# A diffusion layer's token mixer: the rows of a small inverse placed in other slots, one direction's preparation a slot later, the weights' remainders on GpSimd

## The chip, the core and the metric

The kernel runs as one program on one core of a Trainium2 chip. The engines of a core work side by side, each through its own instructions in a fixed order: TensorE (PE; its weight loads are a row of their own, PEld), VectorE (DVE), ScalarE (ACT), GpSimd (POOL) and SyncE (SP), which issues nearly all the DMAs here. The metric is the device time of one execution in microseconds; lower is better. Each variant is timed in several runs, and one execution is also recorded by the profiler.

## The reference, cut to what matters

All data is float32. One layer is computed for 256 latent tokens (x) and 256 context tokens, width 2048:

```
x, cx = LN(alpha*x + 1/2*gate0*SwiGLU_a(mod0(x))),  the same for the context
h   = mod1(x), mod1(cx)
p   = h @ w_in                        # RWKV-7 part (3328 columns) and gMLP part (2048)
for d in (0, 1):                      # forward and backward over the tokens
    S_t = S_{t-1}(diag(w_t) + a_t^T b_t) + v_t^T k_t ;  y_t = S_t r_t     # 16 heads of 64
out = concat(group_norm(y_0 + y_1)..., gMLP(p)) @ w_out
x   = LN(alpha*x + gate1*out);  x = LN(alpha*x + 1/2*gate2*SwiGLU_b(mod2(x)))
```

## The kernel before, in words

The kernel has three long stages: the first SwiGLU, the mixer, the second SwiGLU. Every large product is made of three float32r products: a weight piece `raw` from HBM is rounded on ACT to `whi` (L299), the remainder `wlo` = raw - whi is formed (L302), and TensorE adds whi·h_hi, whi·h_lo and wlo·h_hi (L311 to L313). `wsplit` (L287) does the loading and splitting; a piece is 128x512. There are three `raw` buffers, each of two pieces, and four `whi` and four `wlo` (RAWB, HIB). A list `turn` says who forms `wlo`: with `turn[1]` = 0 always DVE, with 2 every second piece GpSimd, with 1 every piece GpSimd. From the end of the first SwiGLU on and in the mixer's recurrence it is 2; behind the recurrence it is set to 1.

In the mixer the recurrence is done in chunks of 64 tokens by matrices, for a tile t of two heads (eight tiles) and a direction d. The 16 pairs are the units u = 2t + d. The loop over u runs three chains side by side:

- `finish(u)`: `solve`, then for d = 1 group norm and output of the tile. `solve` begins with `pu`, which needs the inverse `R` of its unit (L939); then come `pg` (with `gi`, `wc` on DVE), `pq` (with `qy`), and seven state steps, each a product `pS` on TensorE and an update `S` on DVE (L1004, L1011) that the next one needs.
- `begin(u + 2)`: the preparation of a later unit (`prologue` for d = 0 alone, then `prep`): a scan `pf` on DVE, exponentials `e`, `ei` on ACT, `kd`, `nb`, `bk`, `ar`, `wn` on DVE and `bk`, `ar`, `ac`, `kdx` on GpSimd, products `px`, the masked `aa`, `pt`, `pak`, eight small DMAs to `scr` and one of 1 MB from there to `abc`.
- `inverse(u + 1)`: the inverse of a 64x64 triangle per chunk and head. `small_inverse` makes the 16x16 blocks, row by row: 15 rows, each a product (`a`, L851) and a sum (`x`, L852) on DVE, every row needing the one before. Then `Rt`, `R1`, and the products `pX`, `pR`, `pX2`, `pR2`, with `Z`, `R1`, `R` copied by DVE and ACT between them.

`together` takes one step (up to the next `yield`) of every chain in turn, and after each such pass, a slot, calls `burst`: some of the products still owed for coming tiles (`project`: `pp`; the gMLP's `gmlp_v`: `pgv`, and `gmlp_u`: `pu`; later `wout`: `pwo`) are issued. So a `yield` is where large products may go between steps of the chains. Code that stands in a `behind()` is put after the most recent `urgent` instruction. The order on each engine is then fixed when the program is built; it need not be that of the code.

In a loop pass with d = 1, `finish` takes 13 slots (0 to 12), in one with d = 0 the preparation takes 11 or 12. The lines that the change touches are L734, L853, L859 and, ahead of the loop over u, L1303. Lines behind L734 have numbers higher by 2 or 3 in the changed kernel.

Of the kernel before, what the change touches and what calls it, by code (L numbers as in the profile page):

```python
# [43 lines left out]
def fl(ap):  # L44
    names = " ".join(f"a{i}" for i in range(len(ap.shape) - 1))
    return ap.rearrange(f"p {names} -> p ({names})")
# [7 lines left out]
def tile_layer(ctx: ExitStack, tc: tile.TileContext, x, c, ctx_in, c_ctx, w_ada, b_ada, ln_g, ln_b,  # L54
# [16 lines left out]
    def ps_v(name):  # L71
        return psum.tile([P, 512], F32, tag="v", name=name, bufs=3)
# [7 lines left out]
    def pre(name, shape=(P, 512), dt=F32):  # L80
        return sp.tile(list(shape), dt, tag="pre", name=name, bufs=PRES)
# [7 lines left out]
    def own(name, shape=(P, 512), dt=F32, bufs=1):  # L89
        return sp.tile(list(shape), dt, tag=name, name=name, bufs=bufs)  # L90
# [196 lines left out]
    turn = [0, 0]  # L287
# [413 lines left out]
    def behind():  # L701

        return tc.issue_after(urgent[0].ins) if urgent[0] is not None else nullcontext()
# [11 lines left out]
    def prep(t, d, k, r, kk, vt, ups, kdx, s):  # L715
# [15 lines left out]
        with behind():  # L731
            nc.vector.tensor_reduce(zp[:, :, 0], zp[:, :, 1:L // 2 + 1], axis=AX.X, op=ALU.add, negate=True)
            nc.vector.tensor_tensor_scan(fl(pf), fl(m65), fl(zp), 0.0, op0=ALU.mult, op1=ALU.add)
        yield  # L734
        sgn = -KAPPA if d == 0 else KAPPA
        e = pre("e", (P, NCH, L + 1))
        nc.scalar.activation(fl(e), fl(pf), AF.Exp, scale=sgn)
# [103 lines left out]
    def small_inverse(d, s):  # L841

        x = own("x16", (P, 8, 16), bufs=2)
        sub = own("a16", (P, 8, 16))
        for z in (x, sub):
            nc.scalar.copy(z, i16.unsqueeze(1).to_broadcast([P, 8, 16]))
        for n, i in enumerate(range(14, -1, -1) if d == 0 else range(1, 16)):
            lo, hi = (i + 1, 16) if d == 0 else (0, i)
            r = slice(i, 16) if d == 0 else slice(0, i + 1)
            with behind():  # L850
                nc.vector.tensor_tensor(sub[:, :, lo:hi], x[:, :, lo:hi], s["abc"][:, i, :, lo:hi], op=ALU.mult)  # L851
                nc.vector.tensor_reduce(x[:, :, i], sub[:, :, r], axis=AX.X, op=ALU.add)  # L852
            if n % 4 == 3:  # L853
                yield
        s["x16"] = x

    def inverse(d, s):

        aa = s["aa"]  # L859
        for _ in range(2):  # L860
            yield
        yield from small_inverse(d, s)

        Rt = own("Rt", (P, 8, 32))
        nc.vector.tensor_tensor(Rt.rearrange("p j (b t) -> p j b t", t=16), s["x16"].unsqueeze(2).to_broadcast([P, 8, 2, 16]),
                                mh[:, 0, :].unsqueeze(1).unsqueeze(3).to_broadcast([P, 8, 2, 16]), op=ALU.mult)
        R1 = own("R1", (P, 8, 32))
        nc.vector.transpose(R1, Rt)
        yield
        yield  # L870
        pX = ps_v("pX")
        for i in range(8):
            for b in range(4):
                sb = slice(32 * b, 32 * b + 32)
                nc.tensor.matmul(pX[sb, 32 * i:32 * i + 32], aa[sb, b // 2, i // 4, i % 4, 32 * (b % 2):32 * (b % 2) + 32],
                                 Rt[sb, i, :], start=True, stop=True)
        Z = own("Z", (P, 8, 32))
        urgent[0] = nc.vector.tensor_tensor(Z, pX[:, 0:256].rearrange("p (i t) -> p i t", t=32),
                                ml[d].unsqueeze(1).to_broadcast([P, 8, 32]), op=ALU.mult)
        yield  # L880
        pR = ps_v("pR")
        for i in range(8):
            for b in range(4):
                sb = slice(32 * b, 32 * b + 32)
                nc.tensor.matmul(pR[sb, 32 * i:32 * i + 32], Z[sb, i, :], R1[sb, i, :], start=True, stop=True)
        nc.vector.tensor_tensor(fl(R1), pR[:, 0:256], fl(R1), op=ALU.add)

        Rt = own("Rt", (P, 8, 32))
        nc.vector.transpose(Rt, R1)
        R = own("R", (P, 8, L))  # L890
        nc.vector.tensor_tensor(R.rearrange("p j (b t) -> p j b t", t=32), R1.unsqueeze(2).to_broadcast([P, 8, 2, 32]),
                                mh[:, 1, :].unsqueeze(1).unsqueeze(3).to_broadcast([P, 8, 2, 32]), op=ALU.mult)
        fa, fb = (0, 32) if d == 0 else (32, 0)
        yield
        pX = ps_v("pX2")
        for i in range(8):
            for q in range(2):
                sa, sb = slice(64 * q + fa, 64 * q + fa + 32), slice(64 * q + fb, 64 * q + fb + 32)
                nc.tensor.matmul(pX[sb, 32 * i:32 * i + 32], aa[sa, q, i // 4, i % 4, fb:fb + 32], Rt[sa, i, :],
                                 start=True, stop=True)  # L900
        Z = own("Z", (P, 8, 32))
        for q in range(2):
            sb = slice(64 * q + fb, 64 * q + fb + 32)
            pz = pX[sb, 0:256].rearrange("p (i t) -> p i t", t=32)
            if q:
                nc.scalar.copy(Z[sb], pz)
            else:
                nc.vector.tensor_copy(Z[sb], pz)
        yield
        pR = ps_v("pR2")  # L910
        for i in range(8):
            for q in range(2):
                sa, sb = slice(64 * q + fa, 64 * q + fa + 32), slice(64 * q + fb, 64 * q + fb + 32)
                nc.tensor.matmul(pR[sa, 32 * i:32 * i + 32], Z[sb, i, :], R1[sb, i, :], start=True, stop=True)
        for q in range(2):
            sa = slice(64 * q + fa, 64 * q + fa + 32)
            pz = pR[sa, 0:256].rearrange("p (i t) -> p i t", t=32)
            if q:
                nc.scalar.copy(R[sa, :, fb:fb + 32], pz)
            else:  # L920
                nc.vector.tensor_copy(R[sa, :, fb:fb + 32], pz)
        s["R"] = R
# [348 lines left out]
    def put(g):  # L1271
        queue.append(g)
        return g
# [22 lines left out]
    put(gate_low())  # L1296
    gens[1, 2] = put(project(1, 2))
    together(begin(1), inverse(0, unit[0]))
    begun(1)
    gm = []  # L1300
    for cb in range(4):
        gm += [gmlp_v(cb), gmlp_u(2 * cb), gmlp_u(2 * cb + 1)]
    nu = 2 * NRT  # L1303
    for u in range(nu):
        t, d = u // 2, u % 2
        pace[0] = left[0] / (nu - u + REST) / SLOTS
        if t + 2 < NRT:
            for i in ((0, 2) if d == 0 else (1,)):
                gens[t + 2, i] = put(project(t + 2, i))
            put(gm.pop(0))  # L1310
        if u == 12:
            drain()
            put(tail())
        chains = [finish(u)]
        if u + 2 < nu:
            if d == 0:
                for i in range(3):
                    drain(gens[t + 1, i])
            chains.append(begin(u + 2))
        if u + 1 < nu:  # L1320
            chains.append(inverse((u + 1) % 2, unit[u + 1]))
        together(*chains)
        if u + 2 < nu:
            begun(u + 2)
# [219 lines left out]
```

## Time and profile before

| | us |
|---|---|
| median of three runs | 3366.95 (3363.61 to 3374.13) |
| the profiled execution | 3355.58 |
| its span, from the first to the last instruction | 3353.9 |
| TensorE busy in the span | 3180.8 (95%) |
| VectorE | 2111.1 (63%) |
| ScalarE | 1265.4 (38%) |
| GpSimd | 437.1 (13%) |

The profiled execution was 11.4 us shorter than the median of the runs. Its own time is 1.7 us longer than its span. Busy shares are means over three stages that have different limits; the loop over the units is one part of the span (about 1795 to 2560 us), and what is read of it is read there.

### The profile page before, as it was taken

To read this page: it belongs to the slowest core of one execution; us is meant where nothing else is said; L and a number is where in the kernel's file an instruction comes from. 1 tells how busy PE (TensorE), PEld (TensorE's weight loads), DVE (VectorE), ACT (ScalarE), POOL (GpSimd) and SP (SyncE) were. 2 spreads that over 40 slices of the span, in tenths; PEclk is the share of its full clock that TensorE was granted. 3 is DMA by queue.
4 is the path that set the end of the run, shared out by engine and by line. 5 is a ranking of instruction groups with operands and counts; after the bars stand their busy time and mean duration, and the time that the engine had idled before them with its cause. 6 is when DMAs were issued, how large, how long until landed. Compare 5 with 4: busy or idle time off the path is not lost. (4 is left out here: it accounts for less than half of the span.)

```text
span 3353.9 us, 55585 instructions
## 1 busy us (share of the span) xinstructions
PE 3180.8 (95%) x21224; PEld 2537.6 (76%) x21224; DVE 2111.1 (63%) x4253; ACT 1265.4 (38%) x2225; POOL 437.1 (13%) x393
## 2 busy tenths in 40 slices
PE   8999999999999999999888988898898999999997
PEld 3556877787878878788787777777787888888886
DVE  2345676967557565533867667666776756656568
ACT  2321222222222222222464444544443554444443
POOL 2100000000000000000463333333323000000003
PEclk9999999999999999999988999998898999999999
DMA  8866465757647566433354353434553766666664
GB/s 289 271 201 203 146 177 158 215 168 232 195 145 234 155 192 195 129 94 100 114 158 124 98 120 97 111 97 110 127 128 105 227 209 194 188 189 189 190 188 148
DMA packets 562515, 554.36 MB, mean 165 GB/s; under 512 B 42383, under 2 KB 415284, under 8 KB 560200
## 3 DMA queue, kind: packets, MB, share of 16 engines
q1 hardware_dynamic: 561800, 550.61, 55.0%
q8 instruction: 167, 2.74, 0.3%
q14 instruction: 100, 0.82, 0.1%
q0 software_dynamic: 384, 0.17, 0.0%
q10 hardware_dynamic: 64, 0.02, 0.0%
HBM read 543.35 MB, written 7.35 MB: 164 GB/s over the span
## 5 line engine op out<-in xcount | busy, mean ns | idle before, releaser
L299 ACT CAST whi<-raw 128x512 fp32r<-128x512 f32 (+1 forms) x1366 | 839.4, 618 | 1707.6 <-PE po L312 352.4
L302 DVE TENSOR_TENSOR wlo<-raw,whi 128x512 fp32r<-128x512 f32 (+1 forms) x1188 | 826.2, 698 | 687.8 <-ACT whi L299 678.1
L302 POOL TENSOR_TENSOR wlo<-raw,whi 128x512 fp32r<-128x512 f32 x178 | 240.9, 1356 | 2491.0 <-ACT whi L299 2464.7
L311 PE MATMUL po<-ahi,whi 128*128 128x512 f32 (+1 forms) x768 | 292.6, 381 | 3.8 <-DVE X L417 3.1
L313 PE MATMUL po<-ahi,wlo 128*128 128x512 f32 (+1 forms) x768 | 291.1, 379 | 3.6 <-DVE wlo L302 3.6
L312 PE MATMUL po<-alo,whi 128*128 128x512 f32 (+1 forms) x768 | 292.3, 381 | 0.0
L311 PE MATMUL pgate<-h,whi 128*128 128x512 f32 x704 | 277.9, 395 | 2.0 <-ACT h L307 1.6
L311 PE MATMUL pup<-h,whi 128*128 128x512 f32 x704 | 278.0, 395 | 0.9 <-ACT whi L299 0.9
L313 PE MATMUL pup<-h,wlo 128*128 128x512 f32 x704 | 275.3, 391 | 1.0 <-DVE wlo L302 0.9
L313 PE MATMUL pgate<-h,wlo 128*128 128x512 f32 x704 | 275.1, 391 | 0.2 <-DVE wlo L302 0.2
L312 PE MATMUL pgate<-h,whi 128*128 128x512 f32 x704 | 274.7, 390 | 0.0
L312 PE MATMUL pup<-h,whi 128*128 128x512 f32 x704 | 274.5, 390 | 0.0
L417 DVE SCALAR_TENSOR_TENSOR X<-po,modc,X 128x256 f32<-128x256 f32 x352 | 155.1, 479 | 155.4 <-PE po L313 150.4
L274 DVE SCALAR_TENSOR_TENSOR vt<-xk,wa,vt 128x512 f32<-128x512 f32 x256 | 187.3, 748 | 30.2 <-DMA xk<-in_w_ada_dram 28.5
L311 PEld LDWEIGHTS po<-ahi,whi 128*128 128x128 f32 x768 | 145.9, 190 | 43.3 <-issue 7.7
L274 DVE SCALAR_TENSOR_TENSOR vt<-xv,wa,vt 128x512 f32<-128x512 f32 x224 | 163.7, 748 | 23.2 <-DMA xv<-in_w_ada_dram 21.7
L311 PEld LDWEIGHTS pgate<-h,whi 128*128 128x128 f32 x704 | 132.1, 188 | 53.7 <-ACT whi L299 12.2
L312 PEld LDWEIGHTS po<-alo,whi 128*128 128x128 f32 x768 | 146.0, 190 | 35.2 <-issue 7.5
L311 PEld LDWEIGHTS pup<-h,whi 128*128 128x128 f32 x704 | 132.2, 188 | 51.7 <-ACT whi L299 14.9
L313 PEld LDWEIGHTS po<-ahi,wlo 128*128 128x128 f32 x768 | 146.1, 190 | 33.0 <-DVE wlo L302 4.2
L311 PE MATMUL pp<-h,whi 128*128 128x256 f32 (+1 forms) x448 | 158.6, 354 | 4.1 <-ACT whi L299 2.9
L313 PE MATMUL pp<-h,wlo 128*128 128x256 f32 (+1 forms) x448 | 152.9, 341 | 5.2 <-POOL wlo L302 2.6
(389 smaller groups left out, 6264.0 us busy)
## 6 DMA issues: line engine op xcount, KB each, us to landing
raw<-in_ffn_b_wi_dram SPq DMA_DIRECT2D x176, 512.0 KB
raw<-in_ffn_a_wi_dram SPq DMA_DIRECT2D x156, 512.0 KB
xv<-in_w_ada_dram SPq DMA_DIRECT2D x256, 256.0 KB
xk<-in_w_ada_dram SPq DMA_DIRECT2D x256, 256.0 KB
raw<-in_w_in_dram SPq DMA_DIRECT2D x110, 512.0 KB
raw<-in_ffn_a_wo_dram SPq DMA_DIRECT2D x96, 512.0 KB
raw<-in_ffn_b_wo_dram SPq DMA_DIRECT2D x88, 512.0 KB
abc<-scr SPq DMA_DIRECT2D x16, 1024.0 KB
```

The lines of the kernel that those rows point to most:

```text
L274: nc.vector.scalar_tensor_tensor(acc[v], raw, csil[:, kt, v:v + 1], acc[v], op0=ALU.mult, op1=ALU.add)
L299: nc.scalar.copy(hi, r)
L302: (nc.gpsimd if turn[1] and turn[0] % turn[1] == 0 else nc.vector).tensor_tensor(lo, r, hi.bitcast(F32), op=ALU.subtract)
L311: nc.tensor.matmul(o, wh, ah, start=start, stop=False)
L312: nc.tensor.matmul(o, wh, al, start=False, stop=False)
L313: nc.tensor.matmul(o, wl, ah, start=False, stop=stop)
L417: nc.vector.scalar_tensor_tensor(xs, po[:, sl], gc[:, d:d + 1], xs, op0=ALU.mult, op1=ALU.add)
```

## The change

`small_inverse` gives way after 3, 6, 9 and 12 rows for d = 0, and after 3, 5, 8, 11 and 13 rows for d = 1, where it was after 4, 8 and 12 for both. `inverse` waits three slots ahead of the first row for d = 0 and none for d = 1, where it was two for both. So the rows stand in slots 3 to 7 (d = 0) and 0 to 5 (d = 1) of their loop pass, where they stood in 2 to 5; what follows them starts two slots later for d = 0 and where it was for d = 1. `prep` for d = 1 gives way once more after the scan, so all of it from `e` on comes a slot later. With `turn[1] = 1` ahead of the loop, every `wlo` of the loop is formed by GpSimd.

```diff
@@ prep, behind the scan @@
         yield
+        if d == 1:
+            yield
         sgn = -KAPPA if d == 0 else KAPPA
@@ small_inverse, behind each row @@
-            if n % 4 == 3:
+            if n + 1 in ((3, 6, 9, 12) if d == 0 else (3, 5, 8, 11, 13)):
                 yield
@@ inverse @@
-        for _ in range(2):
-            yield
+        if d == 0:
+            for _ in range(3):
+                yield
         yield from small_inverse(d, s)
@@ ahead of the loop over the units @@
     nu = 2 * NRT
+    turn[1] = 1
     for u in range(nu):
```

The first place is VectorE in the loop pass of unit 4 (d = 0), between its first and second state update `S`; `a` and `x` are the two instructions of a row. Before:

```order
L1011 SCALAR_TENSOR_TENSOR S<-pS,wn,wc 128x64
L851 TENSOR_TENSOR a_17871<-x_17870,abc 128x8x5
L852 TENSOR_REDUCE x_17870<-a_17871 128x8
L851 TENSOR_TENSOR a_17871<-x_17870,abc 128x8x6
L852 TENSOR_REDUCE x_17870<-a_17871 128x8
L851 TENSOR_TENSOR a_17871<-x_17870,abc 128x8x7
L852 TENSOR_REDUCE x_17870<-a_17871 128x8
L851 TENSOR_TENSOR a_17871<-x_17870,abc 128x8x8
L852 TENSOR_REDUCE x_17870<-a_17871 128x8
L732 TENSOR_REDUCE zp<-zp 128x8
L1011 SCALAR_TENSOR_TENSOR S<-pS,wn,wc 128x64
```

And with the change, between the same two updates:

```order
L1014 SCALAR_TENSOR_TENSOR S<-pS,wn,wc 128x64
L732 TENSOR_REDUCE zp<-zp 128x8
L853 TENSOR_TENSOR a_17676<-x_17675,abc 128x8x9
L733 SCALAR_TENSOR_TENSOR pf<-m_96,zp 128x520
L854 TENSOR_REDUCE x_17675<-a_17676 128x8
L853 TENSOR_TENSOR a_17676<-x_17675,abc 128x8x10
L854 TENSOR_REDUCE x_17675<-a_17676 128x8
L1014 SCALAR_TENSOR_TENSOR S<-pS,wn,wc 128x64
```

Two rows stand there instead of four, and eight rows instead of four are done ahead of them; three of those stand at the head of the loop pass, ahead of `gi`. The scan has moved in.

The second place is GpSimd in the loop pass of unit 5 (d = 1), at the preparation of unit 7. Before:

```order
L759 TENSOR_TENSOR ac<-kk,e 128x256
L302 TENSOR_TENSOR wlo<-raw,whi 128x512
L755 TENSOR_TENSOR bk_18518<-kd,ei 128x4x64
L755 TENSOR_TENSOR bk_18519<-kd,ei 128x4x64
L757 TENSOR_TENSOR ar<-kk,e 128x256
L774 TENSOR_TENSOR kdx<-kdx,kd 128x256
```

And with the change:

```order
L761 TENSOR_TENSOR ac<-kk,e 128x256
L302 TENSOR_TENSOR wlo<-raw,whi 128x512 x6
L757 TENSOR_TENSOR bk_18602<-kd,ei 128x4x64
L757 TENSOR_TENSOR bk_18603<-kd,ei 128x4x64
L759 TENSOR_TENSOR ar<-kk,e 128x256
L776 TENSOR_TENSOR kdx<-kdx,kd 128x256
```

Six pieces instead of one stand between `ac`, which needs `e` of ACT, and `bk`, which needs `kd` of DVE.

The third place is TensorE at the end of the loop pass of unit 1 (d = 1), where the inverse of unit 2 ends and `pu` of unit 2 begins the next pass. Before, from the last of the inverse's products:

```order
L914 MATMUL pR_16175<-R_15965,Z 32x32 x15
L313 MATMUL pp<-h_12909,wlo 128x512
L311 MATMUL pp<-h_12961,whi 128x512
L312 MATMUL pp<-h_12962,whi 128x512
L313 MATMUL pp<-h_12961,wlo 128x512
L311 MATMUL pp<-h_12969,whi 128x512
L312 MATMUL pp<-h_12970,whi 128x512
L1092 MATMUL pgb<-ident,y 128x128 x2
L1095 MATMUL pgt<-gl,gup 128x256
L939 MATMUL pu<-rhs,R 64x128 x16
```

And with the change:

```order
L902 MATMUL pX_16157<-Rt,aa 32x32 x16
L1095 MATMUL pgb<-ident,y 128x128 x2
L1098 MATMUL pgt<-gl,gup 128x256
L313 MATMUL pp<-h_12969,wlo 128x512
L311 MATMUL pp<-h_13021,whi 128x512
L917 MATMUL pR_16186<-R_16031,Z 32x32 x16
L312 MATMUL pp<-h_13022,whi 128x512
L313 MATMUL pp<-h_13021,wlo 128x512
L311 MATMUL pp<-h_13029,whi 128x512
L942 MATMUL pu<-rhs,R 64x128 x16
```

Three large products instead of six, and no longer `pgb` and `pgt`, stand between the inverse's last product and `pu`.

## Rows read from the trace of the kernel before

**Rows 1.** The page, part 1: busy time, share of the span and instructions of each engine.

```profile
PE 3180.8 (95%) x21224; PEld 2537.6 (76%) x21224; DVE 2111.1 (63%) x4253; ACT 1265.4 (38%) x2225; POOL 437.1 (13%) x393
```

**Rows 2.** Busy time by stretch of the span. Columns: from and to, length, busy us and instructions of PE, PEld, DVE, ACT and POOL, granted TensorE clock (1.00 is 2.4 GHz), DMA share, GB/s. The first stretch ends ahead of the mixer, the second is the loop over the units, the third begins behind it.

```profile
0.00:1590.00 1590.00, 1563.53 (x6788) 1180.48 (x6789) 915.68 (x1617) 420.63 (x706) 34.70 (x45) 1.00 0.60 184
...
1795.00:2560.00 765.00, 680.77 (x9495) 570.29 (x9494) 528.50 (x1545) 356.07 (x675) 249.95 (x220) 0.94 0.44 111
...
2610.00:3353.90 743.90, 723.93 (x3208) 594.11 (x3206) 470.70 (x709) 354.41 (x583) 29.46 (x21) 0.99 0.62 192
```

**Rows 3.** The same view of 15 stretches of 10 to 25 us in the loop, one in nearly every unit, in which VectorE has hardly a gap: the first, the fourth and the last, and the sum of all 15.

```profile
1815.00:1835.00 20.00, 14.88 (x103) 12.33 (x102) 19.62 (x48) 11.10 (x19) 11.18 (x10) 0.81 0.39 112
...
1960.00:1980.00 20.00, 15.33 (x158) 13.43 (x155) 19.80 (x53) 9.47 (x16) 12.88 (x11) 0.83 0.46 135
...
2500.00:2515.00 15.00, 13.74 (x132) 12.55 (x133) 14.57 (x48) 5.92 (x12) 4.70 (x4) 1.00 0.35 112
sum 285.00, PE 237.16 PEld 202.18 DVE 275.40 ACT 138.77 POOL 133.51; mean PE 15.81 PEld 13.48 DVE 18.36 ACT 9.25 POOL 8.90
```

**Rows 4.** What TensorE waited for in the loop: us in total, times, the longest.

```profile
PE pS L1004 <- DVE S L1011: 13.3, 11, 2.3
PE px L796 <- DVE ar L764: 9.1, 4, 3.1
...
PE pgv L312 <- DVE wlo L302: 4.3, 5, 1.5
...
PE pgv L312 <- POOL wlo L302: 0.4, 2, 0.2
```

**Rows 5.** The sums of the same 15 stretches for three lines alone: L302 on VectorE, L851, L852.

```profile
sum 285.00, DVE 32.43; mean DVE 2.16
...
sum 285.00, DVE 68.50; mean DVE 4.57
...
sum 285.00, DVE 37.45; mean DVE 2.50
```

**Rows 6.** VectorE's groups of instructions in the loop (1795 to 2560 us), costliest first: count, busy us, mean ns of one, idle us before them and what ended it.

```profile
L302 DVE TENSOR_TENSOR wlo<-raw,whi 128x512 fp32r<-128x512 f32 x109 | 83.5, 767 | 73.8 <-ACT whi L299 73.1
L851 DVE TENSOR_TENSOR a<-x,abc 128x8 f32<-128x8 f32 (+14 forms) x225 | 83.2, 370 | 2.3
L852 DVE TENSOR_REDUCE x<-a 128x8 f32<-128x16 f32 (+14 forms) x225 | 49.7, 221 | 2.6
```

**Rows 7.** The same view of GpSimd.

```profile
L302 POOL TENSOR_TENSOR wlo<-raw,whi 128x512 fp32r<-128x512 f32 x110 | 148.5, 1353 | 284.3 <-ACT whi L299 262.5 <-PE pS L1004 10.7 <-issue 5.8
L755 POOL TENSOR_TENSOR bk<-kd,ei 128x256 f32<-128x256 f32 x28 | 24.4, 894 | 31.0 <-DVE kd L744 26.0 <-ACT whi L299 3.4 <-issue 1.6
```

**Rows 8.** The instructions in order of time, VectorE and GpSimd about 1919 us: start, duration in us, engine, line.

```profile
1918.93 0.19 DVE L851 TENSOR_TENSOR a<-x,abc 128x32 f32<-128x32 f32 x1
...
1919.46 1.20 DVE L851 TENSOR_TENSOR a<-x,abc 128x40 f32<-128x40 f32 x1
...
1919.32 1.28 POOL L302 TENSOR_TENSOR wlo<-raw,whi 128x512 fp32r<-128x512 f32 x1 [4.47 <-ACT whi L299]
```

**Rows 9.** Line L851 by itself: count, shortest, median and longest duration in ns, first and last start.

```profile
L851 DVE TENSOR_TENSOR a<-x,abc x225: 159/236/1351, 1814.4 to 2516.5; 128x8 f32<-128x8 f32 x8, 128x24 f32<-128x24 f32 x8, 128x40 f32<-128x40 f32 x8, 128x56 f32<-128x56 f32 x8
```

**Rows 10.** Starts of two neighbouring large products, with 512 columns and with 256: start, duration, line.

```profile
1903.00 0.40 PE L311 MATMUL pp<-h,whi 128*128 128x512 f32 x1
...
1903.24 0.39 PE L312 MATMUL pp<-h,whi 128*128 128x512 f32 x1
...
2274.82 0.28 PE L313 MATMUL pgv<-whi,h 128*128 128x256 f32 x1
2274.94 0.28 PE L311 MATMUL pgv<-whi,h 128*128 128x256 f32 x1
```

**Rows 11.** Busy time by stretch for the four stretches in which `gmlp_v` runs (its first to its last product): the first of them and the sum of all four, and then the sum of L302 on GpSimd alone (8 pieces in each).

```profile
1809.70:1841.20 31.50, 26.21 (x300) 22.23 (x299) 27.88 (x70) 17.73 (x34) 14.94 (x13) 0.84 0.36 103
...
sum 132.10, PE 102.96 PEld 89.67 DVE 106.68 ACT 64.48 POOL 60.94; mean PE 25.74 PEld 22.42 DVE 26.67 ACT 16.12 POOL 15.24
...
sum 132.10, POOL 43.61; mean POOL 10.90
```

**Rows 12.** The end of the loop pass of unit 1: busy time of the stretch from 1885 to 1900 us, and three instructions of VectorE about its end in order of time.

```profile
1885.00:1900.00 15.00, 10.79 (x227) 7.32 (x225) 8.53 (x28) 2.36 (x6) 2.27 (x2) 0.89 0.56 143
...
1897.71 0.41 DVE L921 COPY R<-pR 32x256 f32<-32x256 f32 x1 [0.17 <-PE pR L914]
...
1901.04 0.48 DVE L1097 SCALAR_TENSOR_TENSOR o<-y,pcol,pgt 128x256 f32<-128x256 f32 x1
1901.43 0.42 DVE L1069 TENSOR_TENSOR bon<-pb,xv 128x256 f32<-128x256 f32 x1
```

**Rows 13.** Busy time of the loop pass of unit 1, 13 slots.

```profile
1848.70:1900.80 52.10, 44.86 (x594) 34.73 (x593) 35.25 (x100) 20.29 (x39) 16.39 (x16) 0.97 0.45 108
```

**Rows 14.** The load of `abc` and the first row that reads it, in order of time: of unit 0, and then of unit 3, whose rows run in the loop pass of unit 2.

```profile
1755.38 0.66 SPq L837 DMA_DIRECT2D abc<-scr  x1
...
1768.49 0.16 DVE L851 TENSOR_TENSOR a<-x,abc 128x8 f32<-128x8 f32 x1
...
1886.00 0.63 SPq L837 DMA_DIRECT2D abc<-scr  x1
...
1917.66 0.17 DVE L851 TENSOR_TENSOR a<-x,abc 128x8 f32<-128x8 f32 x1
```

**Rows 15.** What GpSimd waited for in the loop, as in group 4.

```profile
POOL ac L759 <- ACT e L737: 68.7, 10, 18.1
...
POOL bk L755 <- DVE kd L744: 26.0, 10, 5.9
```

## The prediction

> **What bounds the kernel now.** I read the page first: over the span TensorE is busy for 95% and no other engine for more than 63% [rows 1]. That is a mean over stages, so the second view is busy time by stretch. Up to 1590 us and behind 2610 us TensorE has hardly a gap and its full clock; the change touches nothing there. In the loop over the units, 765 us long, it is idle for 84 us and the granted clock is 0.94 [rows 2]. Only these 84 us and what the lower clock costs can be won.
>
> Where in the loop they lie, a finer cut shows: in 15 stretches, 285 us together, VectorE is busy for 275.4 us, and TensorE is idle for 285 - 237.2 = 47.8 us [rows 3]. The granted clock there goes down to 0.81, that is, some of the time TensorE ran at 1.2 and not 2.4 GHz after it had been short of work. From the clock column of all 15 I put that at about 19 us more. So some 67 us of TensorE time are lost where VectorE is full, and VectorE is what to look at. The waits agree: the largest are for the state update `S` and for `ar`, both on VectorE [rows 4].
>
> What fills these stretches: the rows of the small inverse take 68.5 + 37.5 = 106 us of them and remainders 32.4 us [rows 5]; in the loop as a whole 83.2 + 49.7 = 132.9 and 83.5 us [rows 6].
>
> **The change, part by part.** My sum is made against the profiled execution (3355.6 us) and carried over unchanged to the median, which is 11.4 us higher.
>
> *Remainders.* 109 pieces of 767 ns leave VectorE, 83.5 us, of which 32.4 us in the full stretches [rows 5, 6]. On GpSimd one takes 1353 ns [rows 7], so about 109 x 1.353 = 147 us come to its 250 us [rows 2]: it would be busy for 397 of 765 us, 52% instead of 33%. The Trainium skill (GPSIMD Engine Reference, section Engine selection) speaks against this: elementwise work with two inputs belongs on VectorE, GpSimd being about twice as slow. The rows say 1.8 times; by either the engine has room, so the rule alone does not decide.
>
> *What that does to the rows.* A row's product is 0.19 us long when GpSimd rests and 1.20 us when a remainder had begun 0.14 us before it: it ended as the remainder did, near 1920.6 [rows 8]. Over the 225 rows the mean is 370 ns and the median 236 [rows 6, 9], so about 225 x 0.134 = 30 us are spent in such waits. Scaled by GpSimd's busy time (397/250) it becomes 48 us, 18 more. The upper bound lets a row meet a running remainder with chance 0.52 and wait for half of it: 225 x 0.52 x 0.68 = 80 us, 50 more; the lower bound is nothing more, if the rows now stand where GpSimd rests. I take 18, since it is the trace's own rate, and 6 for VectorE's other instructions with two inputs, a third as much.
>
> *Rows moved.* For d = 0 passes eight rows instead of four are done ahead of the second state update, in the part of the pass where TensorE has its longest run of large products; for d = 1 passes six of 15 rows go to slots 6 and 7, behind the crowd. Both come to about four rows fewer in each full stretch: 15 x 4 x 0.59 us (132.9 us by 225) = 35 us. Bounds: nothing, if they meet a full VectorE again, and 53 us for six rows.
>
> *Together* the full stretches lose 32 + 35 - 24 = 43 us of VectorE's 275. If VectorE alone sets their pace, 43 us come off the time. If TensorE's losses only shrink in proportion, it is 43/275 of 67, some 11 us. I take 26, between the two, because TensorE is busy for 83% of these stretches [rows 3] and will soon be the bound itself.
>
> *Supply of pieces.* `gmlp_v` eats fastest: six products of 0.12 us a piece, 0.72 us, against 1.35 for making it on GpSimd [rows 7, 10]. But other work is mixed in. Its four stretches last 132.1 us; GpSimd is busy for 60.9 us of them, 43.6 with half the pieces [rows 11]. With all of them it would be 104.5 us, 79%. That leaves 6.9 us a stretch. A second piece of a `raw` buffer is also read some 0.7 us later than now, and the buffer's next load with it. Price from 0 to 22 us (0.7 us for each of 32 buffers); I take 4, because TensorE has waited 0.4 us for GpSimd's pieces so far [rows 4].
>
> *End of the d = 1 passes.* The inverse for d = 0 now ends in the last slot. Between its last product and `pu` stand three large products of 0.24 us, 0.7 us [rows 10], while VectorE may still have `o` and `bon` before it copies `R`: 0.48 + 0.42 + 0.41 = 1.3 us [rows 12]. That is about 0.6 us for each of seven passes, 4 us; at worst 1.5 us each, some 10. On the other side the same products stood without cover before: from 1885 to 1900 TensorE was idle for 4.2 us [rows 12], and with the state steps gone from those slots some returns. I count 2, from -5 to 10.
>
> *The extra slot of the preparation.* It is a pass of 52.1/13 = 4.0 us [rows 13] for `e`, `ei`, `kd`, `nb`, `bk`, `ar`, `wn`, `px`, `aa`, `pt` and, on SP's queue, for the eight stores to `scr` and the 1 MB load of `abc`. Behind them there SP holds the loads of `raw`; these wait for free buffers, so a slot costs nothing while three buffers are full. `abc` is the thing at risk: its rows come two slots sooner, its load one slot later. The shortest way from load to first row in the trace is 1768.49 - 1755.38 = 13.1 us, and VectorE did not wait; for unit 3 it was 31.7 us [rows 14]. Less 12 us that is about 20, and near 10 at worst, at the head of a pass. If it is late, `gi` is late behind the rows; TensorE has large products there between `pu` and `pg`. Nothing, then; without that cover 3 us in each of seven passes, 21.
>
> Sum: -26 + 4 + 2 = -20 us. 3335.6 for the profiled execution, **3347 us** for the median.
>
> **The rivals.** A difference below 0.3%, 10 us, can't be told from none here.
>
> *The bigger win.* VectorE's crowding goes altogether, and two thirds of the 67 us come back: 45 us, 3322. For it: S, `ar` and `aa` head the waits. Against it: TensorE also waits outside the full stretches, 84 - 47.8 = 36 us, and that stays.
>
> *The rows pay it back: no change.* Every row meets a remainder, as in group 8: 50 us and a third of it for the others, 67 us, are all that the remainders and the moves free (32 + 35). What is left is the 4 and 2 us: about 3370, anywhere from 3360 to 3377. The Trainium skill (SBUF — State Buffer, section Who interferes with whom) states it as a rule: VectorE with two SBUF inputs and GpSimd share a port pair as an exclusive lock, held for a whole instruction, the other blocking until it ends. The two instructions of group 8 agree to 0.1 us. But the rule does not say how often they meet, and so far 30 us are lost where half pieces at 33% would give 225 x 0.33 x 0.68 = 50.
>
> *GpSimd's queue becomes the wait: slower.* GpSimd goes in order, and in the loop it stood at `ac` until `e` came for 68.7 us in 10 waits, and at `bk` until `kd` came for 26.0 in 10 [rows 15], 9.5 us a pass. Now every piece behind is held up too, and TensorE can have no more than four pieces ahead: 2.9 us of `gmlp_v`, 5.8 us of a product with 256 columns, 11 us with 512. That costs 4 x (9.5 - 2.9) = 26 us in the `gmlp_v` stretches and about 8 x (6.9 - 5.8) = 9 in other passes, 35 us: 3347 + 35 = 3382. It decides once TensorE waits for GpSimd's pieces for more than 20 us. For it: the 6.9 us to spare above are less than 9.5. Against it: pieces now stand between `ac` and `bk`, six where one stood, and buffers fill while GpSimd waits.
>
> **How the numbers follow.** Forecast 0.42 (3332 to 3357), the bigger win 0.13, no change 0.20, slower 0.25. So faster 0.55, same 0.20, slower 0.25. The range from 3318 to 3386 leaves out about one in ten on each side and takes in the bounds above.
>
> **What the profile after should show.** No L302 on VectorE in the loop; L302 on GpSimd about 219 times, GpSimd's busy time there near 397 us. The rows' mean from 370 to about 450 ns; above 590 the second rival holds. TensorE's idle time in the loop from 84 to about 65 us and the granted clock above 0.94; waits for `S` and `ar` smaller. TensorE waiting for GpSimd's `wlo` for under 10 us; more, and above all in `pgv`, is the third rival. `pu` waiting for `R` by 0.5 us or so at the head of passes with d = 0. I would be wrong if the loop gets longer than 765 us with VectorE emptier, or if the gain lies outside the loop.

## The result and the profile after

| | before | after |
|---|---|---|
| median of four runs each, taken together, us | 3365.98 | 3402.08 (3398.03 to 3412.45) |
| span of the profiled execution, us | 3353.9 | 3396.3 |
| mean granted clock of TensorE | 0.976 | 0.969 |

The changed kernel takes 1.0111 times as long (95% interval 1.0091 to 1.0131), 36 us more. The forecast was 3347 us, with 3386 as the upper end of its range.

The page, part 1, of the changed kernel answers [rows 1]:

```profile
PE 3194.5 (94%) x21224; PEld 2548.8 (75%) x21224; DVE 2085.3 (61%) x4141; ACT 1263.7 (37%) x2223; POOL 580.1 (17%) x505
```

TensorE has the same 21224 products, yet it is busy for 13.7 us longer, at a granted clock of 0.969 and not 0.976. It is idle for 3396.3 - 3194.5 = 201.8 us where it was 3353.9 - 3180.8 = 173.1, 28.7 more. Together these are the 42.4 us between the two spans, a little more than the 36 between the medians: a trace is one execution, and that of the kernel before was 10 us faster than its median. The stretches show where; columns as in [rows 2]:

```profile
0.00:1590.00 1590.00, 1563.14 (x6778) 1179.79 (x6779) 914.38 (x1616) 419.75 (x705) 34.01 (x44) 1.00 0.60 184
...
1795.00:2560.00 765.00, 652.91 (x8933) 544.04 (x8925) 480.18 (x1368) 340.50 (x648) 366.30 (x310) 0.91 0.42 105
...
2650.00:3396.30 746.30, 726.32 (x3218) 595.97 (x3216) 472.87 (x714) 357.12 (x588) 29.46 (x21) 0.99 0.60 192
```

Ahead of the mixer nothing has changed. In 765 us of the loop TensorE gets through 8933 products, where it was 9495, at a clock of 0.91 and not 0.94; VectorE is emptier by 48 us and GpSimd fuller by 116: a longer loop with VectorE emptier is one of the two signs by which the prediction said it would be wrong. The `pu` of unit 0 starts at 1800.9 us and that of unit 15 at 2570.8, 769.9 us later; before it was 1795.6 and 2530.0, 734.4 us. So 35 us are lost between these two points, and VectorE, which I had taken for the bound, had less to do. The first `pu` is itself 5 us late: it waits 4.55 us for `R`, in the same way as shown below.

What the engines waited for in the loop (1795 to 2600 us, since it is longer now), as in [rows 4], of VectorE and TensorE:

```profile
DVE a L853 <- DMA abc<-scr: 45.6, 8, 7.4
...
PE pu L942 <- DVE R L924: 22.6, 6, 6.8
...
PE pS L1007 <- DVE S L1014: 14.5, 12, 4.6
PE px L798 <- POOL ar L759: 14.3, 7, 4.6
...
PE pgv L312 <- POOL wlo L302: 12.2, 15, 3.4
```

Neither of the first two was there before. Eight times, once for every unit with d = 1, VectorE stands still until the 1 MB of `abc` have come. One of them in order of time (start, duration, engine, line; in brackets the idle time ahead of it and what ended it):

```profile
2219.81 0.62 SPq L839 DMA_DIRECT2D abc<-scr  x1
...
2224.92 0.48 DVE L1096 SCALAR_TENSOR_TENSOR y<-pgb,pcol,bon 128x256 f32<-128x256 f32 x1
...
2232.73 0.17 DVE L853 TENSOR_TENSOR a<-x,abc 128x8 f32<-128x8 f32 x1 [7.32 <-DMA abc<-scr]
2232.84 0.48 DVE L1100 SCALAR_TENSOR_TENSOR o<-y,pcol,pgt 128x256 f32<-128x256 f32 x1
2233.24 0.42 DVE L1072 TENSOR_TENSOR bon<-pb,xv 128x256 f32<-128x256 f32 x1
...
2233.57 0.40 DVE L924 COPY R<-pR 32x256 f32<-32x256 f32 x1
...
2234.03 2.36 PE L942 MATMUL pu<-rhs,R 64*64 64x128 f32 x17 [6.80 <-DVE R L924]
```

The load is issued at 2219.8 and the first row runs 12.9 us later. Behind the row, in VectorE's order, stand `o`, `bon` and the last copy of the previous inverse's `R`, none of which needs `abc`; and `pu`, which opens the pass on TensorE, needs `R`. So a late load for the next unit holds up this one. On top of that TensorE's granted clock is 0.63 from 2230 to 2236 us, that is, for much of this stretch it had 1.2 and not 2.4 GHz: it fell during the 6.8 us in which TensorE was idle and was still low (0.50 from 2234 to 2236 us) when `pu` ran.

The groups of GpSimd and VectorE in the loop (1795 to 2600 us) that answer [rows 6, 7]:

```profile
L302 POOL TENSOR_TENSOR wlo<-raw,whi 128x512 fp32r<-128x512 f32 x218 | 290.7, 1344 | 324.0 <-ACT whi L299 277.7 <-PE pwo L313 22.6 <-issue 6.2
...
L853 DVE TENSOR_TENSOR a<-x,abc 128x8 f32<-128x8 f32 (+14 forms) x225 | 102.8, 457 | 49.0 <-DMA abc<-scr 45.6
```

A row's product takes 457 ns on average, where it was 370 [rows 6]: 20 us more over 225 rows. Without the new remainders (e2 below) it is 341.

### The profile page after: what moved, and what is told of

The parts are those of the page before. It is cut to its first block, busy times and chain, and to the rows that moved or that the text cites. A ratio compares the mean times of both kernels' runs of the same rounds, so it can differ in the third digit from the quotient of the medians.

```text
span 3396.3 us, 55564 instructions
## 1 busy us (share of the span) xinstructions
PE 3194.5 (94%) x21224; PEld 2548.8 (75%) x21224; DVE 2085.3 (61%) x4141; ACT 1263.7 (37%) x2223; POOL 580.1 (17%) x505
## 5 line engine op out<-in xcount | busy, mean ns | idle before, releaser
L302 DVE TENSOR_TENSOR wlo<-raw,whi 128x512 fp32r<-128x512 f32 (+1 forms) x1076 | 740.7, 691 | 609.5 <-ACT whi L299 604.7
L302 POOL TENSOR_TENSOR wlo<-raw,whi 128x512 fp32r<-128x512 f32 x290 | 387.7, 1345 | 2530.7 <-ACT whi L299 2480.9
L311 PEld LDWEIGHTS pgate<-h,whi 128*128 128x128 f32 x704 | 132.1, 188 | 54.1 <-ACT whi L299 11.8
```

What stands on the lines that cost most here:

```text
L302: (nc.gpsimd if turn[1] and turn[0] % turn[1] == 0 else nc.vector).tensor_tensor(lo, r, hi.bitcast(F32), op=ALU.subtract)
L311: nc.tensor.matmul(o, wh, ah, start=start, stop=False)
```

## The experiments

Two theories. **A (the load):** the loss comes from `abc`, which is late since the rows of d = 1 start two slots sooner. **B (GpSimd):** it comes from the remainders on GpSimd, by holding VectorE (an instruction of VectorE stands until one of GpSimd ends, as in [rows 8]) or as a queue. Each ratio is against the kernel before on the same chip in the same hours (its median there was 3358 to 3361 us).

### One part at a time: e1, e2, e3, e5

e1 takes the rows of d = 1 back to their old slots, e2 puts every second remainder back on VectorE, e3 is the kernel before with the remainders alone changed, e5 is the changed kernel with the load of `abc` cut in two.

```diff
e1, against the changed kernel
-            if n + 1 in ((3, 6, 9, 12) if d == 0 else (3, 5, 8, 11, 13)):
+            if n + 1 in ((3, 6, 9, 12) if d == 0 else (4, 8, 12)):
-        if d == 0:
-            for _ in range(3):
-                yield
+        for _ in range(3 if d == 0 else 2):
+            yield
e2, against the changed kernel
-    turn[1] = 1
e3, against the kernel before
+    turn[1] = 1
e5, against the changed kernel: the half with the first rows goes first
-        nc.sync.dma_start(abc.rearrange("p s j t -> p (s j t)"),
-                          scr.rearrange("(g s) c -> g (s c)", g=8).unsqueeze(1).to_broadcast([8, 16, 2048]))
+        for h in ((0, 1) if d else (1, 0)):
+            nc.sync.dma_start(abc[:, 8 * h:8 * h + 8].rearrange("p s j t -> p (s j t)"),
+                              scr.rearrange("(g s) c -> g (s c)", g=8)[:, 1024 * h:1024 * h + 1024].unsqueeze(1).to_broadcast([8, 16, 1024]))
```

e1: 

> The changed kernel, with the rows of the small inverse for d = 1 placed as before (two slots of waiting, then 4, 8, 12); the rest of the change stays (d = 0 rows in slots 3 to 7, the extra slot of the preparation, all remainders on GpSimd). Theory A, the late abc load: in the changed kernel VectorE waited 45.6 us in 8 waits for the load of abc at the first row of the d = 1 inverses, with the copy of R behind it, and TensorE 22.6 us for R. With two slots (8 us) more no first row waits; the 22.6 us and the slow clock behind them come back, 25 to 32 of the 36 us: 3370 to 3377. Theory B, GpSimd's queue: the rows of d = 1 matter little; at most 8 us come back: 3394 or more.

e2: 

> The changed kernel with every second remainder of the loop on VectorE again, so only the rows' slots and the extra slot of the preparation are changed. Theory A: the first rows of the d = 1 inverses still wait for abc, 40 us or more on VectorE in sum, and TensorE still waits for R by some 20 us: 3385 to 3400. Theory B: TensorE's 12.2 us of waits for remainders in pgv and 14.3 us for ar of GpSimd go, and with them most of the loss: 3366 to 3375.

e3: 

> The kernel before with all remainders of the loop on GpSimd, nothing else changed. Theory A: no first row waits for abc; VectorE loses 83 us of work and gets some 20 us more of waits for the port back, TensorE waits for GpSimd's pieces by some 10 us: 3355 to 3372, no clear difference to before. Theory B: the loss is here: 3385 to 3402.

e5: 

> The changed kernel with the 1 MB load of abc as two loads of 512 KB, the half whose rows come first ahead; no step is moved. Theory A: the first row waits for half the data only. The load now takes 12 to 15 us from its issue to the first row; if some 9 of these are the transfer, the first half is there about 4 us sooner, VectorE's waits for abc fall from 45.6 us to 10 to 20, TensorE's for R from 22.6 to under 10, and the time to 3380 to 3392. If the wait is not the transfer but the way there, it stays at 3400. Theory B: no difference, 3395 to 3405.

Measured: e1 1.0063 (1.0045 to 1.0080), e2 1.0078 (1.0049 to 1.0108), e3 1.0045 (1.0021 to 1.0069), e5 1.0054 (1.0037 to 1.0072). Neither theory has it alone. e2 has none of the new remainders and loses 26 us, with the waits of the late load whole:

```profile
DVE a L853 <- DMA abc<-scr: 45.4, 8, 7.6
...
PE pu L942 <- DVE R L924: 33.6, 7, 6.8
PE px L798 <- POOL ar L759: 8.4, 6, 3.8
```

e5 and e1, each of which takes that wait away in another way, give back 19 and 16 us of the 36. In e5, in order of time, the first row runs 6.6 us after the issue of the two loads (one row of the view for both), and `pu` has 0.24 us to wait:

```profile
2201.38 1.27 SPq L840 DMA_DIRECT2D abc<-scr  x2
...
2207.94 0.17 DVE L854 TENSOR_TENSOR a<-x,abc 128x8 f32<-128x8 f32 x1 [0.76 <-DMA abc<-scr]
...
2209.23 0.97 PE L943 MATMUL pu<-rhs,R 64*64 64x128 f32 x10 [0.24 <-DVE R L925]
```

And e3, where no load is late, loses 15 us by the remainders alone. There TensorE's wait for the state update has doubled (13.3 us in 11 before, [rows 4]):

```profile
PE pS L1004 <- DVE S L1011: 27.3, 16, 4.3
```

The longest of these waits, in order of time on GpSimd, VectorE and TensorE:

```profile
2483.75 2.67 POOL L302 TENSOR_TENSOR wlo<-raw,whi 128x512 fp32r<-128x512 f32 x2
2484.00 1.23 DVE L769 TENSOR_TENSOR wn<-e,ei 128x7 f32<-128x7 f32 x1
2485.15 0.15 DVE L770 TENSOR_TENSOR wn<-e,ei 128x1 f32<-128x1 f32 x1
2485.22 1.24 DVE L851 TENSOR_TENSOR a<-x,abc 128x8 f32<-128x8 f32 x1
2486.38 0.27 DVE L1011 SCALAR_TENSOR_TENSOR S<-pS,wn,wc 128x64 f32<-128x64 f32 x1
...
2486.70 0.48 PE L1004 MATMUL pS<-S,gi 64*64 64x64 f32 x4 [4.31 <-DVE S L1011]
```

Two remainders run on GpSimd back to back, and each catches one tiny instruction of VectorE with two inputs: a `wn` of seven columns takes 1.23 us where one of one column takes 0.15, and a first row of eight takes 1.24 where the one of the changed kernel above took 0.17. Both stand ahead of `S`, and TensorE waits for it: by the shorter durations just named (1.23 - 0.15 and 1.24 - 0.17) some 2.1 of these 4.31 us are holds, an estimate. The holds that the prediction added as 18 us over 225 rows, under 0.1 us each, are a full remainder long where they fall on the chain. The rule of the Trainium skill that the prediction cites (SBUF — State Buffer, section Who interferes with whom), by which the other engine blocks for a whole instruction, agrees with these two.

### Does the extra slot make the load late: e4

```diff
against the changed kernel
-        if d == 1:
-            yield
```

> The changed kernel without the extra slot of the second direction's preparation; rows and GpSimd's remainders as changed. Theory L (the load of abc is late behind the first row): the load is issued one slot, about 4 us, sooner, so the eight waits of VectorE for abc at the head of the d = 1 passes fall from 45.6 us in all to about 45.6 - 8 x 4 = 14 us, TensorE's wait of pu for R goes from 22.6 us to under 8, and the time comes down by about 15 to 20 us: ratio to the kernel before near 1.005 to 1.007. Rival M (the rows themselves, two slots sooner in d = 1 passes, crowd VectorE where o, bon and R stand): the waits for abc shrink but the time stays within 5 us of the changed kernel, ratio 1.010 to 1.012.

Measured: 1.0140 (1.0103 to 1.0178), no better than the changed kernel, and the waits as they were:

```profile
DVE a L851 <- DMA abc<-scr: 45.1, 8, 7.8
```

Theory L missed here. From the issue of the load to the waiting row it is still 11.7 to 15.6 us, in the changed kernel 12.2 to 14.8: the first row follows the landing of the load in both. It is the rows' being two slots sooner that makes the load late (e1 keeps the slot and has no such wait), not the slot. Why a load that is prepared one slot sooner isn't there sooner for its row, these runs don't show.

### The rows alone, with an early load: e6, and the load alone: e12

e6 is e2 with the cut load, e12 the kernel before with it; the edits are those of e2 and e5 above.

e6: 

> The changed kernel with every second remainder back on VectorE, and the load of abc cut in two halves of which the one with the first rows goes first: the rows' new slots and the extra slot alone, with abc early. Theory L: the +26 us of the rows and the slot were the late load; with it early what is left is what the spread of the rows is worth in itself, between 0 and -10 us: ratio 0.997 to 1.001. Rival M: the rows cost by where they stand, ratio 1.004 to 1.008 with few waits for abc left.

e12: 

> The kernel before with abc loaded in two halves, nothing else. Theory L: VectorE waited for no load of abc in it, so nothing is to be had: ratio 0.9985 to 1.0015, and what the rows with the load cut gained (0.9958) is the rows' own. Rival: the cut load helps by itself, for example the loads of raw behind it; ratio 0.996 to 0.998, and then the rows' new slots are worth nothing.

Measured: e6 0.9958 (0.9938 to 0.9977), e12 0.9991 (0.9976 to 1.0006). So cutting the load gives nothing clear of noise by itself. With every second remainder on VectorE, the rows' new slots with the extra slot are worth 14 us once `abc` is early; with the one load they cost 26. The late load therefore costs some 40 us there (e2 against e6). In e6 the wait for `S` is half of what it was, as the forecast wanted it, and that for `R` is gone:

```profile
PE pS L1008 <- DVE S L1015: 6.4, 12, 1.2
...
PE pu L943 <- DVE R L925: 0.2, 1, 0.2
```

### How long a hold is: e8, e9, e13

A remainder on GpSimd is cut into instructions of 128x256, in e8 (all of them on GpSimd, as e3) and e9 (every second one, as before), and of 128x128 in e13 (as e3).

```diff
-            (nc.gpsimd if turn[1] and turn[0] % turn[1] == 0 else nc.vector).tensor_tensor(lo, r, hi.bitcast(F32), op=ALU.subtract)
+            if turn[1] and turn[0] % turn[1] == 0:
+                w = lo.shape[2] // 2
+                for c in (slice(0, w), slice(w, 2 * w)):
+                    nc.gpsimd.tensor_tensor(lo[:, :, c], r[:, :, c], hi.bitcast(F32)[:, :, c], op=ALU.subtract)
+            else:
+                nc.vector.tensor_tensor(lo, r, hi.bitcast(F32), op=ALU.subtract)
```

e8: 

> The kernel before with all the remainders of the loop on GpSimd (it was 15 us slower so), each remainder there cut into two instructions of 128x256. Theory P (a remainder on GpSimd holds a VectorE row, and the state update S behind it, for up to its whole 1.28 us): the hold is halved, the rows' mean falls from 469 to about 400 ns or less, TensorE's wait of pS for S from 27 us toward 18, and about half of the 15 us comes back: ratio near 1.002. Rival Q (GpSimd is too slow a supplier of pieces): a second instruction adds its own start to each piece, GpSimd is busy for longer, the waits for GpSimd's wlo grow from 3.8 us, and the time goes up: ratio 1.006 or more. Rival O (the order of TensorE's products, which moved with the engine of the remainders, makes the loss): no change, ratio 1.004 to 1.005, with the wait of pS for S still near 27 us.

e9: 

> The kernel before, every second remainder on GpSimd as there, but cut into two instructions of 128x256. Theory P: the rows' excess of about 34 us over their unheld length falls to about 20, S comes sooner, and the time comes down by up to 5 to 8 us: ratio 0.997 to 0.999. Rival Q: more work on GpSimd, ratio 1.000 to 1.003. Rival O: 1.000.

e13: 

> All remainders of the loop on GpSimd, each in four instructions of 128x128 (two gave 0.9976, one 1.0045). Theory P alone: a hold is half as long again, the rows' mean goes from 355 to about 300 ns, and the waits of pS for S under 10 us. But a half took 780 ns against 1344 for the whole, so each instruction has a start of its own of some 200 ns, four of them take about 2 us, GpSimd would be busy for about 560 of the loop's 765 us, and TensorE's waits for GpSimd's wlo go from 13 to 30 us or more: ratio 0.999 to 1.005, slower than in halves.

Measured: e8 0.9976 (0.9961 to 0.9991), e9 0.9974 (0.9959 to 0.9989), e13 1.0008 (0.9992 to 1.0025). Two halves take 23 us off e3 and make it faster than the kernel before. The groups of e8 (1795 to 2600 us):

```profile
L305 POOL TENSOR_TENSOR wlo<-raw,whi 128x256 fp32r<-128x256 f32 x452 | 340.5, 780 | 247.3 <-ACT whi L299 221.7 <-issue 11.6 <-PE pS L1009 8.3
...
L856 DVE TENSOR_TENSOR a<-x,abc 128x8 f32<-128x8 f32 (+14 forms) x225 | 79.8, 355 | 3.3
```

Two waits of TensorE in e8, of the view of waits:

```profile
PE pgv L317 <- POOL wlo L305: 13.3, 10, 3.6
PE pS L1009 <- DVE S L1016: 12.9, 8, 3.4
```

GpSimd works longer (340.5 us for its remainders, 293.9 in e3), a row's mean falls from 469 in e3 to 355 ns, and the wait for `S` from 27.3 to 12.9 us. GpSimd's total work rises, and TensorE's wait for its pieces too (13.3 us, 3.8 in e3), while the time falls: that speaks against the queue as e3's cause. The order of TensorE's products was built anew in each kernel; that part of it also moved the time isn't excluded, but the row's mean and the wait for `S` moved as the hold does. Quarters show the other end: rows of 337 ns and 9.0 us of waits for `S`, but remainders of 410.4 us on GpSimd, which is now late with the pieces:

```profile
PE pgv L317 <- POOL wlo L305: 19.4, 15, 3.5
...
PE pS L1009 <- DVE S L1016: 9.0, 5, 2.6
```

### Both cures: e10, e11, e14

e10 is the changed kernel with the cut load and the halves, e11 the same with every second remainder on VectorE, e14 the changed kernel with the halves alone; the edits are those of e2, e5 and e8.

e10: 

> The whole change with both suspected causes taken away: abc loaded in two halves, and each remainder on GpSimd cut into two instructions of 128x256. Theory L+P (the late load and the long holds are all that the change lost by): the sum of what the halves gave alone (1.0045 to 0.9976 with all remainders on GpSimd, -0.7%) and of the changed kernel with the load cut (1.0054): 0.9985; and if the rows' new slots are worth what they gave with every second remainder on GpSimd (0.9958), together with the halves (0.9976) 0.993. Rival: something else in the change still costs, for example eight more dear passes or GpSimd as a supplier; ratio over 1.002, with waits for GpSimd's wlo above 15 us.

e11: 

> The rows' new slots and the extra slot, abc loaded in two halves, every second remainder on GpSimd as before but in two instructions of 128x256. Theory L+P: the gains of the two kernels add up, 0.9958 and 0.9974: ratio 0.993. Rival (both gains come out of the same idle time of TensorE): 0.995 to 0.996, no better than the rows with the load cut.

e14: 

> The changed kernel with GpSimd's remainders in two instructions of 128x256, abc still in one load. Theory L+P (two causes that add up): the halves take off what they took with the load cut (1.0054 to 1.002) or more, up to the 0.7% they took from the remainders alone: ratio 1.004 to 1.008, with the waits for abc of 45 us still there. Rival: the late load hides the holds, since VectorE rests anyway: 1.010 to 1.012.

Measured: e11 0.9920 (0.9897 to 0.9943), 3330 us, the fastest of all; e10 1.0020 (1.0005 to 1.0034); e14 1.0123 (1.0098 to 1.0148). In e11 the gains of e6 and e9 add up, as expected. e14 missed: the halves give nothing while the load is late; VectorE, less held, waits longer at the row instead (50.7 us in 7, 45.6 in the changed kernel). Its waits:

```profile
DVE a L858 <- DMA abc<-scr: 50.7, 7, 9.3
...
PE pu L947 <- DVE R L929: 29.9, 6, 7.3
```

e10 is the rival's case: with the late load and the long holds taken away, the whole change is still 1.0% slower than e11, where every second remainder stays on VectorE. Two waits behind GpSimd are larger there than in e11 (whose `ar` row is 11.9 us, `wlo` 3.8):

```profile
PE px L803 <- POOL ar L764: 17.1, 7, 3.9
PE pgv L317 <- POOL wlo L305: 14.0, 14, 3.4
```

### What is left of the loss: e15, e16, e17

e15 is e10 with the products `bk` and `ar` of the preparation on VectorE, e16 is e10 without the extra slot, e17 is e11 without it.

```diff
e15, against e10
-            nc.gpsimd.tensor_tensor(bk[q][:, :, 1 - q, :], kdv[:, :, q, :], eiv[:, :, q, :], op=ALU.mult)
+            nc.vector.tensor_tensor(bk[q][:, :, 1 - q, :], kdv[:, :, q, :], eiv[:, :, q, :], op=ALU.mult)
-        nc.gpsimd.tensor_tensor(ar[:, 0], c64(kk)[:, 4:8], eprev[:, 4:8], op=ALU.mult)
+        nc.vector.tensor_tensor(ar[:, 0], c64(kk)[:, 4:8], eprev[:, 4:8], op=ALU.mult)
```

e15: 

> The whole change with abc loaded in two halves and the remainders in halves (1.002), and the three products bk, bk and ar of each preparation on VectorE and not on GpSimd. Theory G (GpSimd's queue: these products come behind remainders there, and TensorE's px waits for ar): px's wait of 17.1 us in 7 goes below 8, though VectorE's chain of bk, bk, ar grows by three products of some 0.41 us; ratio 0.997 to 1.000. Rival H (the two engines hold each other, so that bk and ar take 0.9 us on either while both work on them): VectorE's own three are then quicker by as much as it has more to do, and px comes at the same time: ratio 1.001 to 1.003.

e16: 

> The whole change with abc in two halves and the remainders in halves (1.002), without the extra slot of the second direction's preparation. Theory S (the slot makes ar, px and aa late, and what is left of the loss with them): px's waits shrink from 20 us toward 9, ratio 0.996 to 0.999. Rival G: the slot doesn't matter, 1.001 to 1.003.

e17: 

> The rows' new slots, abc in two halves, every second remainder on GpSimd in halves (0.992), without the extra slot. Theory S: the slot costs there too: ratio 0.988 to 0.990. Rival: the slot keeps the preparation out of the crowd and is worth something; 0.993 to 0.996. If it doesn't matter: 0.991 to 0.993.

Measured: e15 1.0027 (1.0010 to 1.0044), e16 1.0011 (0.9995 to 1.0028), e17 0.9962 (0.9952 to 0.9973). In e15 the wait only changed its name:

```profile
PE px L803 <- DVE ar L771: 26.3, 11, 5.7
```

So neither the queue of `bk` and `ar` on GpSimd nor the extra slot explains e10. With every second remainder on VectorE the slot is even worth 0.4% (e11 against e17). Put side by side, the ratios show that the two parts of the change don't simply add up:

| | every second remainder on GpSimd | all on GpSimd |
|---|---|---|
| old slots, one load | 1 (the kernel before) | 1.0045 (e3) |
| new slots, one load | 1.0078 (e2) | 1.0111 (the changed kernel) |
| new slots, load cut | 0.9958 (e6) | 1.0054 (e5) |
| old slots, one load, halves | 0.9974 (e9) | 0.9976 (e8) |
| new slots, load cut, halves | 0.9920 (e11) | 1.0020 (e10) |

In the left column the new slots with an early load gain 14 us, and with halves 18. In the right column they gain nothing (e5 against e3) and with halves they lose some 15 us (e10 against e8). In the old slots, once cut in halves, all the remainders can go to GpSimd at no price (e8 against e9); in the new slots they cost 34 us (e10 against e11). What the new slots and a full GpSimd do to each other stays open. Something of it is told by the stretches of the loop (1795 to 2560 us), of e10 and then of e11:

```profile
1795.00:2560.00 765.00, 679.58 (x9348) 567.20 (x9344) 459.24 (x1394) 348.18 (x664) 417.55 (x527) 0.90 0.41 107
...
1795.00:2560.00 765.00, 694.74 (x9604) 580.17 (x9604) 516.93 (x1561) 360.38 (x683) 279.87 (x340) 0.94 0.43 114
```

In e10 TensorE is idle for 85.4 us, hardly more than the 84.2 of the kernel before [rows 2], but its granted clock is 0.90 and not 0.94 (more of the time at 1.2 and less at 2.4 GHz), and it gets through 147 products fewer. So in these two traces e10's loss against the kernel before lies in the clock; they are 21 us apart, though, where by the ratio of the runs it is 7 us. Against e11 it lies in 15 us more of idle time and the clock. What lowers the clock at the same idle time, these runs don't settle.

## Why the prediction was wrong, point by point

**The extra slot and `abc`: the step that failed first.** It named the risk, put the load at "near 10" us ahead of its row "at worst" against 13.1 from load to row, priced it at 21 us, and then struck it out: "If it is late, `gi` is late behind the rows; TensorE has large products there between `pu` and `pg`." The cover was the wrong one. It looked at what needs the rows, and not at what stands behind the waiting instruction on the same engine: `o`, `bon` and the copy of `R` for the unit whose `pu` is next. The loads were late in all eight units, by 5.7 us in the mean. Price measured: 19 us in the changed kernel (against e5), some 40 with the remainders left alone (e2 against e6). So the struck-out 21 was the right size for the whole change, but only half of the price with the remainders left alone. The cause is the move of the rows and not the slot (e1, e4).

**Crowding, -26.** Of its parts, the remainders left VectorE as counted, GpSimd made 218 pieces at 1344 ns (147 us was the estimate for the added half; its busy time in 805 us rose from 267.6 to 389.1), and the rows' mean of 457 ns is the 450 forecast. What failed is the conversion of VectorE's time into time of the kernel. VectorE is busy for 26 us less over the span (2085.3 and 2111.1) and the kernel takes 36 longer; and a hold of 1.2 us ahead of `S` is time that TensorE waits (27.3 us for `S` in e3, 13.3 before). In the new slots the remainders double that wait as well, from 6.4 us (e6) to 13.1 (e5); the 14.5 of the changed kernel must be held against these 6.4 and not against the 13.3 of before. So the remainders alone, which by the forecast free 32 us of VectorE in the full stretches less 24 for holds, brought not a small gain but 15 us of loss (e3), and turned to a small gain once a hold was half as long (e8). The second rival took the same view: it, too, summed the holds on VectorE. The sum was fine (457 ns a row), but their place on the chain of `S` was not looked at.

**The rows moved: right in kind, for one half of the cases.** With the load early and every second remainder on VectorE they bring 14 us (e6; the cut load alone brings nothing measurable, e12), with smaller waits for `S`, as the forecast described. With all remainders on GpSimd, as in the change, they bring nothing even with an early load (e5 against e3). The sum added the two parts as if each were worth the same with or without the other.

**Supply of pieces, +4.** TensorE's wait for GpSimd's `wlo` in `pgv` went from 0.4 to 12.2 us, above the "under 10" named, inside the 0 to 22. Missed altogether: `ar`, made by GpSimd, for which `px` waits 14.3 us. In part that is the third rival's mechanism, with the preparation as its victim and not only the pieces; but 8.4 us of it are there without the new remainders (e2), and curing the queue did not help (e15), so it isn't shown to have cost time.

**End of the d = 1 passes, +2.** `pu` does wait for `R`, by 22.6 us in 6, not by the 0.6 us of `o` and `bon` each: they weren't the length that mattered, but what they had to wait behind.

**Range.** 3386 was too low. The dearest rival put a single loss, 35 us by GpSimd's queue, on a forecast that had 20 us of gain in it (3382), and the late load stood in no rival. Here the gain did not come, and two losses came together: 26 us by the rows with their late load (e2) and 15 by the remainders (e3), 41 where the whole change lost 36.

## What to carry to other kernels

When work is moved sooner, look at what stands behind it in the same engine's order, and check that its data, the DMAs above all, come as much sooner; a wait is paid by whoever is queued behind it, not by whoever reads its result. When work goes to GpSimd beside a VectorE that carries a chain of small instructions, the length of one GpSimd instruction matters more than its sum: cut it until its supply becomes the limit (here in two, not four). And test each part of a change of several parts alone, and then in pairs: here a part that is worth 14 us by itself, once its load is early, is worth nothing next to another.

## What the runs showed of the hardware

- A remainder on GpSimd takes 1344 ns in one instruction, two of 780 in halves, four of 489 in quarters, holds included: 1.34, 1.56 and 1.96 us for the same 128x512. In halves the 0.22 us more were worth it (e8 against e3), in quarters the 0.62 us were not (e13 against e8).
- The hold goes both ways: at 1835 us of e10 an `ar` on VectorE takes 0.90 us beside an `ar` of the same size on GpSimd that takes 0.86. GpSimd's fastest `ar` in this trace takes 0.67, and VectorE's `Rt`, as large, 0.41 right behind.

```profile
1835.16 0.90 DVE L771 TENSOR_TENSOR ar<-xr,e 128x256 f32<-128x256 f32 x1
1835.74 0.86 POOL L764 TENSOR_TENSOR ar<-kk,e 128x256 f32<-128x256 f32 x1
...
1836.55 0.41 DVE L874 TENSOR_TENSOR Rt<-x,mh 128x256 f32<-128x256 f32 x1
```

- The load of 1 MB from `scr` took 12.2 to 14.8 us in the changed kernel from its issue to the row that waited for it; with two loads of half the size, issued 0.6 us apart, the rows that waited in e5 ran 6.5 to 7.2 us after the first issue (up to 11.8 in e17).
- Part of the loss came with a lower clock and not as idle time: a third in the changed kernel (13.7 of 42.4 us), half in e3, whose trace has TensorE busy for 16 us more and idle for 15 more than before, with the same products.
